# Partition sums of the sub-norms and of five row norms: from TensorE to GpSimd

## The chip, the cores and the metric

The kernel runs on one core of one Trainium2 chip. The metric is the device time of an execution in microseconds. A run is one execution; the times before are those of three runs, and the profile is of one more execution.

## What is computed

One layer of a decoder with 1024 tokens (rows) of width 2048. It is cut here to what the change touches; the projections, the stick-breaking heads and the rotary embedding are left out.

```python
def rmsnorm(x, g, eps=NORM_EPS):
    xf = x.astype(jnp.float32)
    y = xf * lax.rsqrt(jnp.mean(xf * xf, axis=-1, keepdims=True) + eps)
    return (y * g.astype(jnp.float32)).astype(x.dtype)
...
    hn = rmsnorm(h, norm_mix_g[i])
    proj = hn @ w_in[i]
...
    df_out = differential_attention(dq, dk, df_v.reshape(B, S, DF_HEADS, DF_V_DIM), lam)
    df_out = rmsnorm(df_out, subln_g[i], SUBLN_EPS) * (1.0 - lambda_init)
...
    h = h + mixed @ w_out[i]
    gate = jax.nn.sigmoid(rmsnorm(h, norm_ple_g[i]) @ w_ple_gate[i])
    h = h + gate * (p[i] @ w_ple_proj[i])
return rmsnorm(h, norm_final_g)
```

The norm behind the attention (the sub-norm) is over the 128 values of one head; the three row norms are over the 2048 values of a row.

## The kernel before

Data lies transposed: a tile has 128 features on the partitions and 512 tokens (a half of the sequence) on the free dimension. So a sum over the features of a token is a sum over partitions. Every product is done with operands split into a high and a low part (`F32R`), as three matmuls: high x high, high x low, low x high. Low parts are made by DVE as `value - high`, after ACT has cast the value to its high part.

The stages, in order: the value and gate projections of all heads (class `Seven`, `gv`); then 32 units, 16 heads for the first half of the tokens (`half = 1` in the code) and 16 for the second (`half = 0`). Differential and stick-breaking heads alternate, so there are 8 differential heads in each half. A unit projects q and k of its head (L295 to L297) while the attention of the head before runs between these matmuls. Then the output projection (`op`), the gate projection and the embeddings, and the last norm.

TensorE's instructions are kept in the order in which the program writes them; so are those of ScalarE and VectorE from L867 on. Where the attention's steps fall among the matmuls of a unit is set by the table `TICK` (L41): `side.tick()` (L264) advances one tick for each three matmuls and runs what is due. Weights for the products of `Seven` are made ahead into a ring of ten tiles (`WRING`, L654). GpSimd (POOL) issues DMAs, among them the stores of low weight parts of the first half (L197), and does a few small operations; it takes them one after the other.

The sums over partitions are products with `onesr`, a 128x128 matrix of 1/128 (L87 to L89), which leave the mean of the 128 partitions on every partition:

- Sub-norm of a differential head: `squared` (L567) squares the head's output on ACT and makes the high part `sqh`; `low` (L576) makes the low part `sql` on DVE. Some ten ticks later `norm` (L585) does two matmuls into `msq`, then `roots` takes the logarithm and the exponential on ACT and `step` refines on DVE. 8 heads, 2 halves.
- First row norm: `split_sum`, `total`, `root` and `refined` (L1153 to L1180) at slots given in `joint` (L1191), one for each half.
- Norm ahead of the gate, and the last norm of one half: the rows' squares are collected in DRAM, `load_sums` (L1938) reads them, `norm` (L1918) sums over partitions; three times (L2013, L2093, L2222).
- The last norm of the other half uses `ones` in `mean` and `mean_t` (L2282, L2289).

`scale_rope` (L1304) multiplies the tables of the rotary embedding by the row norm, on DVE for the first half and on POOL for the second.

## Time and profile before

| what | value |
|---|---|
| median of 3 runs | 2303.81 us (2303.38 to 2305.9) |
| the profiled execution, its own time | 2303.42 us |
| span of that execution | 2301.2 us |
| busy: PE, DVE, ACT, POOL | 99%, 79%, 58%, 14% of the span |
| instructions on PE, POOL | 10945, 500 |
| DMA, mean | 246 GB/s |

Busy time of PE is a modelled one, since matmuls are pipelined: the recorded durations of matmuls overlap, and the distance between starts is what one costs. Spans on POOL are rough. In the rows below PE is TensorE, DVE VectorE, ACT ScalarE and POOL GpSimd; L588 is line 588 of the kernel; times are in us, those of a single operation in the tile and line views in ns.

### The profile page before, as it was taken

The numbers are of one execution on the slowest core, as the hardware profiler recorded it, in microseconds if no ns is written. First come the engines' busy times: TensorE is split into PE (matmuls) and PEld (weight loads), VectorE is DVE, ScalarE is ACT, GpSimd is POOL, SyncE is SP. The second block draws the span as 40 slices with busy tenths as digits, with TensorE's granted clock in tenths as the row PEclk, the third lists the DMA queues.
The fourth block names the chain that finished last, engine by engine and source line by source line (L and its number), as shares of the span: only waits on it lengthen the run. The fifth ranks groups of instructions, "written<-read, shape, count | busy, mean of one in ns | idle before, by whom it ended". The sixth has DMA issues, their size and how long they took to land. (4 is left out here: it accounts for less than half of the span.)

```text
span 2301.2 us, 32625 instructions
## 1 busy us (share of the span) xinstructions
PE 2286.1 (99%) x10945; PEld 1914.5 (83%) x10945; DVE 1817.6 (79%) x3155; ACT 1337.4 (58%) x2418; POOL 322.1 (14%) x500
## 2 busy tenths in 40 slices
PE   9999999999999999999999999999999999999998
PEld 7888888888888888888888888888888888888887
DVE  6588887777768888878777878778787988687787
ACT  6424354444467777778777777777633435532555
POOL 2121111111211111101011001111121121111000
PEclk9999999999999999999999999999999999999999
DMA  7687677776798888899677667778898788998975
GB/s 268 212 303 262 209 246 228 235 216 197 236 298 260 245 257 249 258 293 307 202 207 201 170 219 210 202 211 247 249 220 247 248 247 276 320 355 267 303 254 188
DMA packets 291260, 565.06 MB, mean 246 GB/s; under 512 B 63746, under 2 KB 74242, under 8 KB 291092
## 3 DMA queue, kind: packets, MB, share of 16 engines
q1 hardware_dynamic: 220276, 383.35, 52.6%
q0 software_dynamic: 58864, 158.10, 25.1%
q10 hardware_dynamic: 11952, 21.53, 2.6%
q8 instruction: 86, 1.41, 0.3%
q14 instruction: 82, 0.67, 0.1%
HBM read 359.17 MB, written 203.69 MB: 245 GB/s over the span
## 5 line engine op out<-in xcount | busy, mean ns | idle before, releaser
L805 ACT CAST wpr<-T 128x512 fp32r<-128x512 f32 x208 | 127.6, 620 | 428.2 <-DVE T L764 363.2
L295 PE MATMUL acc<-xh,whi 128*128 128x512 f32 x768 | 309.7, 403 | 0.0
L296 PE MATMUL acc<-xl,whi 128*128 128x512 f32 x768 | 300.6, 391 | 0.0
L297 PE MATMUL acc<-xh,wlo 128*128 128x512 f32 x768 | 300.5, 391 | 0.0
L297 PEld LDWEIGHTS acc<-xh,wlo 128*128 128x128 f32 x768 | 144.2, 188 | 31.3
L295 PEld LDWEIGHTS acc<-xh,whi 128*128 128x128 f32 x768 | 144.7, 188 | 25.1
L296 PEld LDWEIGHTS acc<-xl,whi 128*128 128x128 f32 x768 | 144.8, 189 | 24.2
L805 ACT CAST wpr<-wraw 128x512 fp32r<-128x512 f32 x128 | 78.5, 617 | 120.7 <-DMA wraw<-w_vg 36.1
L819 DVE TENSOR_TENSOR wpr<-T,wpr 128x512 fp32r<-128x512 f32 x208 | 142.4, 684 | 5.9 <-ACT wpr L805 5.1
L200 ACT CAST whi<-wraw 128x1024 fp32r<-128x1024 f32 x128 | 134.1, 1048 | 11.1 <-DMA wraw<-w_in 7.1
L520 DVE TENSOR_TENSOR awl<-tp,awh 128x256 fp32r<-128x256 f32 (+1 forms) x160 | 92.6, 579 | 36.2 <-ACT awh L515 35.6
L443 ACT ACTIVATE et<-z,mx 128x512 f32<-128x512 f32 (+7 forms) x128 | 95.0, 742 | 39.1 <-DVE mx L435 38.5
L435 DVE CUSTOM_DVE_ANT_0 z<-z,wide 128x512 f32<-128x512 f32 (+7 forms) x128 | 97.6, 764 | 25.0 <-PE z L388 22.8
L710 PE MATMUL pbc<-cA,wpr 128*128 128x512 f32 x480 | 115.6, 390 | 0.2 <-DVE u L1256 0.2
L710 PE MATMUL pc<-cS,wpr 128*128 128x512 f32 x480 | 115.3, 389 | 0.0
L710 PE MATMUL pbc<-cS,wpr 128*128 128x512 f32 x480 | 115.3, 389 | 0.0
L710 PEld LDWEIGHTS pbc<-cA,wpr 128*128 128x128 f32 x480 | 90.0, 188 | 19.7 <-DVE u L1256 1.1
L710 PEld LDWEIGHTS pc<-cS,wpr 128*128 128x128 f32 x480 | 90.1, 188 | 18.7
L710 PEld LDWEIGHTS pbc<-cS,wpr 128*128 128x128 f32 x480 | 90.1, 188 | 18.7
L710 PE MATMUL pbc<-cS2h,wpr 128*128 128x512 f32 x320 | 105.3, 390 | 0.0
L710 PE MATMUL pc<-cS4h,wpr 128*128 128x512 f32 x320 | 105.0, 389 | 0.0
L918 POOL DMA_DIRECT2D vg_d<-hc x96 | 62.5, 651 | 291.1 <-DVE hc L1144 163.4
(555 smaller groups left out, 6453.0 us busy)
## 6 DMA issues: line engine op xcount, KB each, us to landing
wraw<-w_in SPq DMA_DIRECT2D x128, 512.0 KB, 5.0
wraw<-w_vg SPq DMA_DIRECT2D x143, 256.0 KB, 3.9
wlo_d<-wlo POOLq DMA_DIRECT2D x56, 512.0 KB, 6.6
vg_d<-hc POOLq DMA_DIRECT2D x96, 256.0 KB, 4.3
wlo<-wlo_d SPq DMA_DIRECT2D x48, 512.0 KB, 3.9
wraw<-w_gate SPq DMA_DIRECT2D x92, 256.0 KB, 5.3
h_d<-hc POOLq DMA_DIRECT2D x56, 256.0 KB, 5.3
wraw<-w_out SPq DMA_DIRECT2D x56, 256.0 KB, 4.5
```

Source lines behind the costliest of these rows:

```text
L200: side.later(1, lambda: A.copy(hi[:, o], raw[:, o]))
L295: T.matmul(acc[c], hi[:, k2, kh, c, :], xh, start=first, stop=False)
L296: T.matmul(acc[c], hi[:, k2, kh, c, :], xl, start=False, stop=False)
L297: T.matmul(acc[c], lo[k2][:, kh, c, :], xh, start=False, stop=last)
L435: V.tensor_tensor_reduce(z[:, vw], z[:, vw], add, -DF_SCALE, 3.0e38, ALU.add, ALU.min, mx)
L443: A.activation(et[:, vw], z[:, vw], AF.Exp, bias=mx[:, 0:1], scale=-1.0, accum_out=l[:, c:c + 1])
L520: V.tensor_tensor(wl[:, o, :], tp[:, o, :], wh[:, o, :].bitcast(F32), op=ALU.subtract)
L710: T.matmul(o, a[:, w], x, start=start and k + i == 0, stop=k == 3 and i == 2, skip_group_check=True)
L805: A.copy(t[:, 0], src)
L819: V.tensor_tensor(t[:, 1], src, t[:, 0].bitcast(F32), op=ALU.subtract)
L918: G.dma_start(vg_d[hf, blk, u], o, **(dict(accum_op=ALU.add) if ph else {}))
```

## The change

The squares of a head's output, the sums of squares of the first row norm and those of three later row norms go as they are to `partition_all_reduce` on POOL, which leaves the sum on every partition of a tile in SBUF. No high and low parts are made of them, and the scale by 1/128 moves into the logarithm and the refinement. The mean of the last norm's other half (`mean`, `mean_t`) stays on TensorE. `scale_rope` runs on DVE for both halves. `TICK` and the slots are the same, but for `total`, which stands where `split_sum` stood (slots 71 and 72).

```diff
--- before.py
+++ after.py
@@ -6,6 +6,7 @@
 import numpy as np
 
 import concourse.bass as bass
+import concourse.bass_isa as bass_isa
 import concourse.tile as tile
 from concourse import mybir
 from concourse import bacc as _bacc
@@ -18,6 +19,7 @@
 AF = mybir.ActivationFunctionType
 ALU = mybir.AluOpType
 AX = mybir.AxisListType
+RED = bass_isa.ReduceOp
 
 P = 128
 D = 2048
@@ -569,32 +571,27 @@
                 sq = ev.tile([P, HALF], F32, name="sqv", tag="xt", bufs=4)
                 A.activation(sq, both, AF.Square)
                 V.scalar_tensor_tensor(sg, both, subg[:, 0:1], sg, op0=ALU.mult, op1=ALU.mult)
-                sqh = ev.tile([P, HALF], F32R, name="sqh", tag="xt", bufs=4)
-                A.copy(sqh, sq)
-                sqs[0] = both, sq, sqh
-
-            def low():
-                both, sq, sqh = sqs[0]
-                sql = ev.tile([P, HALF], F32R, name="sql", tag="xt", bufs=4)
-                V.tensor_tensor(sql, sq, sqh.bitcast(F32), op=ALU.subtract)
-                sqs[0] = both, sq, sqh, sql
+                sqs[0] = both, sq
+
+            def summed_squares():
+                both, sq = sqs[0]
+                msq = ev.tile([P, HALF], F32, name="msq", tag="xt", bufs=4)
+                G.partition_all_reduce(msq, sq, P, RED.add)
+                sqs[0] = both, sq, msq
 
             side.later(tk("squared")[0], squared)
-            side.later(tk("squared")[1], low)
+            side.later(tk("squared")[1], summed_squares)
 
         def norm():
-            rs_, t, sqh, sql = sqs[0]
-            msq = pp.tile([P, HALF], F32, name="msq", tag="t")
-            T.matmul(msq, onesr, sqh, start=True, stop=False)
-            T.matmul(msq, onesr, sql, start=False, stop=True)
+            rs_, t, msq = sqs[0]
 
             def roots():
-                A.activation(rs_, msq, AF.Ln, bias=eps5[:, 0:1], scale=1.0)
+                A.activation(rs_, msq, AF.Ln, bias=eps5[:, 0:1], scale=1.0 / P)
                 A.activation(rs_, rs_, AF.Exp, scale=-0.5)
 
             def step():
-                V.scalar_tensor_tensor(t, msq, SUB_EPS, rs_, op0=ALU.add, op1=ALU.mult)
-                V.scalar_tensor_tensor(t, t, -0.5, rs_, op0=ALU.mult, op1=ALU.mult)
+                V.scalar_tensor_tensor(t, msq, SUB_EPS * P, rs_, op0=ALU.add, op1=ALU.mult)
+                V.scalar_tensor_tensor(t, t, -0.5 / P, rs_, op0=ALU.mult, op1=ALU.mult)
                 V.scalar_tensor_tensor(rs_, t, 1.5, rs_, op0=ALU.add, op1=ALU.mult)
                 V.tensor_tensor(sg, sg, rs_, op=ALU.mult)
                 mixed(half, hd, sg)
@@ -1148,23 +1145,16 @@
             else:
                 vput(o, ph, hf, blk, u)
 
-        rstds, halves, totals = {}, {}, {}
-
-        def split_sum(hf):
-            high, low = halves[hf] = [ev.tile([P, HALF], F32R, name=nm, tag="xt", bufs=4) for nm in ("ssah", "ssal")]
-            A.copy(high, ssa[hf])
-            V.tensor_tensor(low, ssa[hf], high.bitcast(F32), op=ALU.subtract)
+        rstds, totals = {}, {}
 
         def total(hf):
-            ps = totals[hf] = pp.tile([P, HALF], F32, name="ssps", tag="acc", bufs=2)
-            high, low = halves[hf]
-            T.matmul(ps, onesr, high, start=True, stop=False)
-            T.matmul(ps, onesr, low, start=False, stop=True)
+            totals[hf] = ev.tile([P, HALF], F32, name="total", tag="xt", bufs=4)
+            G.partition_all_reduce(totals[hf], ssa[hf], P, RED.add)
 
         steps = {}
 
         def root(hf):
-            A.activation(ssa[hf], totals[hf], AF.Ln, bias=eps6[:, 0:1], scale=1.0 / NK)
+            A.activation(ssa[hf], totals[hf], AF.Ln, bias=eps6[:, 0:1], scale=1.0 / D)
             A.activation(ssa[hf], ssa[hf], AF.Exp, scale=-0.5)
             rstds[hf] = ssa[hf]
 
@@ -1173,9 +1163,9 @@
                 steps[hf] = ev.tile([P, HALF], F32, name="nt", tag="xt", bufs=4)
             t, ps, r = steps[hf], totals[hf], ssa[hf]
             if i == 0:
-                V.scalar_tensor_tensor(t, ps, EPS * NK, r, op0=ALU.add, op1=ALU.mult)
+                V.scalar_tensor_tensor(t, ps, EPS * D, r, op0=ALU.add, op1=ALU.mult)
             elif i == 1:
-                V.scalar_tensor_tensor(t, t, -0.5 / NK, r, op0=ALU.mult, op1=ALU.mult)
+                V.scalar_tensor_tensor(t, t, -0.5 / D, r, op0=ALU.mult, op1=ALU.mult)
             else:
                 V.scalar_tensor_tensor(r, t, 1.5, r, op0=ALU.add, op1=ALU.mult)
 
@@ -1188,7 +1178,7 @@
                 rturned[hf] = const.tile([P, 4], F32, name=f"rturned{hf}", tag=f"rturned{hf}")
                 nc.sync.dma_start(rturned[hf], r_d[hf].rearrange("(j p) -> p j", p=P))
 
-        joint = {71: partial(split_sum, 1), 72: partial(split_sum, 0), 74: lambda: (total(1), total(0)), 75: partial(root, 1)}
+        joint = {71: partial(total, 1), 72: partial(total, 0), 75: partial(root, 1)}
         joint.update({76 + i: partial(refined, 1, i) for i in (0, 2)})
         joint[77] = lambda: (refined(1, 1), root(0))
         joint.update({79 + i: partial(refined, 0, i) for i in range(3)})
@@ -1302,7 +1292,7 @@
             return cs
 
         def scale_rope(hf, cs):
-            (V if hf else G).tensor_tensor(cs, cs, rstds[hf].unsqueeze(1).to_broadcast([P, 2, HALF]), op=ALU.mult)
+            V.tensor_tensor(cs, cs, rstds[hf].unsqueeze(1).to_broadcast([P, 2, HALF]), op=ALU.mult)
 
         for hf in range(2):
             rcols[hf] = const.tile([P, 2, 4], F32, name=f"rcol{hf}", tag=f"rcol{hf}")
@@ -1917,20 +1907,17 @@
 
         def norm(tiles):
 
-            out, high, low = tiles
-            ps = pp.tile([P, HALF], F32, name="ssps", tag="t")
-            T.matmul(ps, onesr, high, start=True, stop=False)
-            T.matmul(ps, onesr, low, start=False, stop=True)
+            out, ps = tiles[0], tiles[2]
 
             def roots():
                 A.preload_act_table_set("natural_log_exp_and_others")
-                A.activation(out, ps, AF.Ln, bias=eps6[:, 0:1], scale=1.0 / NK)
+                A.activation(out, ps, AF.Ln, bias=eps6[:, 0:1], scale=1.0 / D)
                 A.activation(out, out, AF.Exp, scale=-0.5)
 
             def step():
                 t = at.tile([P, HALF], F32, name="nt", tag="sg", bufs=3)
-                V.scalar_tensor_tensor(t, ps, EPS * NK, out, op0=ALU.add, op1=ALU.mult)
-                V.scalar_tensor_tensor(t, t, -0.5 / NK, out, op0=ALU.mult, op1=ALU.mult)
+                V.scalar_tensor_tensor(t, ps, EPS * D, out, op0=ALU.add, op1=ALU.mult)
+                V.scalar_tensor_tensor(t, t, -0.5 / D, out, op0=ALU.mult, op1=ALU.mult)
                 V.scalar_tensor_tensor(out, t, 1.5, out, op0=ALU.add, op1=ALU.mult)
 
             op.soon.extend([(op.slot + 1, roots), (op.slot + 2, step)])
@@ -1938,15 +1925,14 @@
         def load_sums(half, tags):
             r = []
             for i, (pool, tag, n) in enumerate(tags):
-                r.append(pool.tile([P, HALF], (F32, F32R)[i], name="sums", tag=tag, bufs=n))
-                nc.sync.dma_start(r[i].bitcast(F32), sq_d[half, i])
+                r.append(pool.tile([P, HALF], F32, name="sums", tag=tag, bufs=n))
+                nc.sync.dma_start(r[i], sq_d[half, i])
 
             def split():
-                total, high = r
-                V.tensor_tensor(total, total, high.bitcast(F32), op=ALU.add)
-                r.append(at.tile([P, HALF], F32R, name="suml", tag="sg", bufs=3))
-                A.copy(high, total)
-                V.tensor_tensor(r[2], total, high.bitcast(F32), op=ALU.subtract)
+                total, more = r
+                V.tensor_tensor(total, total, more, op=ALU.add)
+                r.append(at.tile([P, HALF], F32, name="mean", tag="sg", bufs=3))
+                G.partition_all_reduce(r[2], total, P, RED.add)
 
             op.soon.append((op.slot + TICK["sumlag"], split))
             return r
```

On POOL, at the first differential head of the first half (`msq` is the sum, `sqv` the squares, `wlo_d` the store of low weight parts, `k_d`, `kl_d` and `v_d` stores of keys and values). Before:

```order
L483 DMA v_d<-v 128x1024
L1610 DMA v_10751<-v_d 128x1024
L197 DMA wlo_d<-wlo 128x1024 x3
L1513 DMA k_d<-k 256x1x512
L1515 DMA kl_d<-kl 128x512
L197 DMA wlo_d<-wlo 128x1024 x2
L483 DMA v_d<-v 128x1024
L1513 DMA k_d<-k 256x1x512
L197 DMA wlo_d<-wlo 128x1024
```

And now:

```order
L485 DMA v_d<-v 128x1024
L1600 DMA v_10701<-v_d 128x1024
L199 DMA wlo_d<-wlo 128x1024 x2
L579 ISA msq<-sqv 128x512
L199 DMA wlo_d<-wlo 128x1024
L1503 DMA k_d<-k 256x1x512
L1505 DMA kl_d<-kl 128x512
L199 DMA wlo_d<-wlo 128x1024 x2
L485 DMA v_d<-v 128x1024
L1503 DMA k_d<-k 256x1x512
L199 DMA wlo_d<-wlo 128x1024
```

The reduction stands ahead of the last of three stores of low weight parts, and with it ahead of the stores of keys that follow.

On DVE, in the same place (`lead` and `awl` are the low parts of the attention weights that PE reads next, `wlo` the low weight part of the projection). Before:

```order
L1592 TENSOR_TENSOR qk<-qk,cs 128x512
L1579 TENSOR_TENSOR q<-qk,q 64x512
L398 TENSOR_TENSOR z<-z,masks 128x128
L579 TENSOR_TENSOR sql<-sqv,sqh 128x512
L1593 TENSOR_TENSOR qk<-qk,sw 128x512
L196 TENSOR_TENSOR wlo<-wraw,whi 128x1024
L1579 TENSOR_TENSOR q<-qk,q 64x512
L418 SCALAR_TENSOR_TENSOR pt<-pt 128x255
L519 TENSOR_TENSOR lead<-tp,lead 128x128
L520 TENSOR_TENSOR awl<-tp,awh 128x256
```

And now:

```order
L1582 TENSOR_TENSOR qk<-qk,cs 128x512
L1569 TENSOR_TENSOR q<-qk,q 64x512
L400 TENSOR_TENSOR z<-z,masks 128x128
L1583 TENSOR_TENSOR qk<-qk,sw 128x512
L198 TENSOR_TENSOR wlo<-wraw,whi 128x1024
L1569 TENSOR_TENSOR q<-qk,q 64x512
L420 SCALAR_TENSOR_TENSOR pt<-pt 128x255
L521 TENSOR_TENSOR lead<-tp,lead 128x128
L522 TENSOR_TENSOR awl<-tp,awh 128x256
```

The subtraction for `sql` is gone; the rest keeps its order. On ACT the cast for `sqh` goes in the same way, and the logarithm of `msq` stands where it stood.

On PE, at the same head, before:

```order
L387 MATMUL z<-k,q 128x512
L388 MATMUL z<-kl,qz 128x512
L588 MATMUL msq<-sqh,onesr 128x512
L589 MATMUL msq<-sql,onesr 128x512
L295 MATMUL acc_6239<-xh_5573,whi 128x512
L296 MATMUL acc_6239<-xl_5574,whi 128x512
```

The two rows with `onesr` are gone now, and their neighbours follow each other.

## Rows read from the trace of the kernel before

**Rows 1.** The page, first part: busy time, share of the span, instructions of each engine.

```profile
PE 2286.1 (99%) x10945; PEld 1914.5 (83%) x10945; DVE 1817.6 (79%) x3155; ACT 1337.4 (58%) x2418; POOL 322.1 (14%) x500
```

**Rows 2.** Waits of PE: line, waited for, us in total, times, longest.

```profile
PE av L543 <- DVE awl L520: 1.9, 4, 0.9
```

**Rows 3.** Tiles msq and ssps: count, ns min/median/max, first and last start, shape.

```profile
L588 PE MATMUL msq<-sqh,onesr x16: 389/389/501, 711.9 to 1659.3; 128*128 128x512 f32 x16
...
L1922 PE MATMUL ssps<-sums,onesr x3: 389/389/390, 1959.0 to 2208.4; 128*128 128x512 f32 x3
...
L1161 PE MATMUL ssps<-ssah,onesr x2: 389/389/389, 296.4 to 296.8; 128*128 128x512 f32 x2
```

**Rows 4.** Timeline of PE around a pair: start, us, engine, line, operation.

```profile
1164.10 0.39 PE L588 MATMUL msq<-sqh,onesr 128*128 128x512 f32 x1
...
1164.55 0.39 PE L295 MATMUL acc<-xh,whi 128*128 128x512 f32 x1
```

**Rows 5.** Lines 1305, 475, 1324 and 197, each by itself: count, ns min/median/max.

```profile
L1305 POOLq MODIFY_POOL_CONFIG  x2: 37/37/37, 1029.0 to 1029.1; - x2
...
L1305 DVE TENSOR_TENSOR cs<-cs,ssa x1: 1216/1216/1216, 635.0 to 635.0; 128x1024 f32<-128x1024 f32 x1
...
L475 POOL COPY vw<-vf x2: 778/998/1218, 1040.9 to 1041.6; 128x512 uint16<-128x512 uint16 x2
...
L1324 DVE SCALAR_TENSOR_TENSOR xl<-xl,gvec,xh x16: 719/749/851, 1030.3 to 1061.2; 128x512 fp32r<-128x512 f32 x16
...
DMA to landing us min/median/max: 4.8/6.6/9.3
```

**Rows 6.** Timeline of POOL: its add, and its two copies; idle time before, releaser.

```profile
1035.82 2.41 POOL L1305 TENSOR_TENSOR cs<-cs,ssa 128x1024 f32<-128x1024 f32 x1 [6.78 <-DMA cs<-rope]
...
1040.93 1.89 POOL L475 COPY vw<-vf 128x512 uint16<-128x512 uint16 x2 [1.51 <-PE msq L589]
```

**Rows 7.** Timeline of DVE in the same stretch.

```profile
1037.92 0.85 DVE L1324 SCALAR_TENSOR_TENSOR xl<-xl,gvec,xh 128x512 fp32r<-128x512 f32 x1 [1.36 <-ACT xh L1323]
...
1041.34 0.85 DVE L1324 SCALAR_TENSOR_TENSOR xl<-xl,gvec,xh 128x512 fp32r<-128x512 f32 x1 [0.72 <-ACT xh L1323]
```

**Rows 8.** Timeline of ACT, first differential head of the first half.

```profile
698.38 0.64 ACT L570 ACTIVATE sqv<-avb 128x512 f32<-128x512 f32 x1
...
712.83 0.69 ACT L592 ACTIVATE avb<-msq,eps 128x512 f32<-128x512 f32 x1
```

**Rows 9.** Timeline of DVE, the same head.

```profile
698.85 0.69 DVE L1579 TENSOR_TENSOR q<-qk,q 64x512 fp32r<-64x512 f32 x1
...
700.39 0.68 DVE L1593 TENSOR_TENSOR qk<-qk,sw 128x512 f32<-128x512 f32 x1
...
703.57 0.27 DVE L519 TENSOR_TENSOR lead<-tp,lead 128x128 fp32r<-128x128 f32 x1
```

**Rows 10.** Timeline of PE, the same head.

```profile
703.89 0.51 PE L538 MATMUL av<-lead,v 128*128 128x256 f32 x2
```

**Rows 11.** Timeline of ACT, first differential head of the second half.

```profile
1152.88 0.63 ACT L570 ACTIVATE sqv<-avb 128x512 f32<-128x512 f32 x1
...
1164.75 0.69 ACT L592 ACTIVATE avb<-msq,eps 128x512 f32<-128x512 f32 x1 [1.16 <-PE msq L589]
```

**Rows 12.** Timeline of DVE, the same head.

```profile
1159.80 0.81 DVE L422 TENSOR_TENSOR bt<-pt,bt 128x639 f32<-128x639 f32 x1
...
1162.68 0.69 DVE L520 TENSOR_TENSOR awl<-tp,awh 128x512 fp32r<-128x512 f32 x1 [2.06 <-ACT awh L515]
```

**Rows 13.** Timeline of PE, the same head.

```profile
1166.15 0.28 PE L543 MATMUL av<-awl,v 128*128 128x256 f32 x1
```

**Rows 14.** Timeline of POOL, first half: a store of a low weight part.

```profile
702.50 0.53 POOL L197 DMA_DIRECT2D wlo_d<-wlo  x1 [7.71 <-DVE wlo L196]
```

**Rows 15.** Timeline of DVE, first half: the later write of the low part.

```profile
712.96 1.23 DVE L196 TENSOR_TENSOR wlo<-wraw,whi 128x1024 fp32r<-128x1024 f32 x1
```

## The prediction

> **What bounds the kernel now.** I read the page's first part before anything else: TensorE (PE) is busy 2286.1 us of a span of 2301.2 us, VectorE (DVE) 79%, ScalarE (ACT) 58%, GpSimd (POOL) 14% [rows 1]. Then the waits of PE: ten rows of a few tenths to 1.9 us, and the largest is a wait for a DVE operation [rows 2]. So nothing holds PE back by more than some microseconds in all; a matmul taken out of its order shortens the kernel by that matmul, as long as whatever takes its place does not make PE wait. The profiled execution took 2303.42 us, 0.39 under the median of the runs, 2303.81. The sum below is made against 2303.4, and I take a change of under 0.2% (4.6 us) as no change, about what a measurement of this kernel can tell.
>
> **What is removed.** The tile views name the matmuls with the matrix of ones: 16 pairs for the sub-norms (L588 and L589: 8 heads, twice), 3 pairs for the row norms (L1922, L1923) and 2 pairs for the first ones (L1161, L1162) [rows 3]. That is 42 matmuls of 512 columns. Their recorded 389 ns overlap each other; what one costs PE is the distance to the next start. From the first of a pair at 1164.10 to the matmul behind the pair at 1164.55 there are 0.45 us for two [rows 4], so 0.23 us each with the rounding of the rows, and 42 x 0.23 = **9.7 us** off PE. The order listing confirms that these 42 are gone and that nothing comes in their place on PE. The 21 casts on ACT and 21 subtractions on DVE that made the high and low parts go too. They gain nothing by themselves: neither engine is the bound [rows 1, 2].
>
> **What is added.** 21 reductions over partitions on POOL, 128x512 in float32, which I call R, with a duration T. No row of the trace shows one, so T is bounded by the compute operations that POOL does have. One add of 128x1024 took 2.41 us [rows 6], so 1.2 us for 512 columns, and the faster of two copies of 128x512 took 0.78 us [rows 5]. Lower bound: R reads and writes its data once at the rate of that add, T = 1.2. Upper bound: 128 partitions are 2^7, and R does seven rounds of a move and an add, 7 x (1.2 + 0.8) = 14.0. I take seven adds with the moves hidden, T = **8.4**: it lies nearest to the add's row, which is the only float32 row, and a tree of seven steps is the least arithmetic that 128 values need one after another. The Trainium skill's page "GPSIMD Engine Reference", section 3.2, gives 247,699 ns for a reduction along the partition axis of 128x2048, another instruction than R; a quarter of it, an estimate of 61.9 us, would make the sum below some 880 us, and no row here shows it.
>
> **What else moves.** The scaling of the rope tables for the second half goes from POOL to DVE: 1.22 us there, as its twin of the first half shows [rows 5], at a place where DVE sat idle 1.36 us [rows 7]; nothing, and 1.2 us if that idle time has moved. The code load that POOL did before its add (L1305's MODIFY_POOL_CONFIG, at 1029.0 [rows 5]) now stands ahead of the first R, near 286 us. Its price is between 0 and the 6.8 us that POOL sat idle behind it, an idle time whose releaser was a DMA [rows 6]; I take 0, since the row blames the DMA.
>
> **Where R stands in time.** In the first half (seven of the eight heads, and the eighth behind the seam alike) the squares end at 698.38 + 0.64 = 699.0, and the logarithm that needs the sum stands on ACT at 712.83 [rows 8]: 13.8 us. In the second half the squares end at 1153.5, the logarithm is at 1164.75 [rows 11]: 11.2 us. With T = 8.4 the result is in time in both, so ACT does not wait. What remains is what R does to its neighbours while it runs.
>
> **The neighbour that decides: DVE.** Three rows around 1040 us show POOL and DVE in each other's way. The operation at L1324 reads two tensors from SBUF and takes 0.749 us in the median of 16; the two that started while POOL computed are the longest, 0.85 [rows 5, 7]. The first began 0.31 us before POOL's add ended, the second inside POOL's pair of copies [rows 6]. Of these two equal copies one took 778 ns and one 1218 [rows 5], and the DVE operation ends at 1042.19, 0.6 us ahead of the pair's end at 1042.82: the longer copy looks as if it had waited for DVE. So a read by POOL and a DVE operation with two SBUF inputs seem to take turns, each for its whole length. The Trainium skill's page "SBUF — State Buffer", section "Who interferes with whom", says just that: the pair of ports that both use is an exclusive lock, a VectorE instruction with two SBUF inputs contends with a GpSimd instruction that reads SBUF, and the one that starts second blocks fully. By that rule R, if it reads as it goes, stops such DVE operations for all of T. Without the rule the sum would be the 9.7 us gained and nothing else.
>
> First half: the operation at L1579, with two SBUF inputs, ends at 699.54, and R gets its turn. The next such operation, L1593, stands at 700.39 (a little earlier now, without the subtraction ahead of it), and from its start to the end of the lead tile's low part at 703.57 + 0.27 = 703.84 DVE needs 3.45 us [rows 9]. PE takes that tile at 703.89 [rows 10]: there is no slack. If L1593 starts only at 699.54 + T, PE is late by 699.54 + T + 3.45 - 703.89 = T - 0.9, so 7.5 us for T = 8.4, and 8 x 7.5 = **60 us**. The bounds: 8 x 0.3 = 2.4 at T = 1.2, and 8 x 13.1 = 105 at T = 14.0.
>
> Second half: R starts at 1153.5 and ends at 1161.9. The next DVE operation with two inputs that bears on PE is L422 at 1159.80 (0.81 us); behind it stands the low part at 1162.68 (0.69 us) [rows 12], which PE reads at 1166.15 [rows 13]. L422 at 1161.9 gives a low part that is done by 1161.9 + 0.81 + 0.69 = 1163.4: in time, **0**. At T = 14.0 it is done at 1169.0, 2.9 late, 8 x 2.9 = 23.
>
> The five R of the row norms: between 0 and 5 x 7.5 = 38. I take 0, because weight parts for those products are made ahead, in a ring of ten tiles.
>
> **Queued behind R on POOL** stand DMA issues. In the second half it is the load of keys for a later head. In the first half it is the store of low weight parts at 702.50 [rows 14], which lands 6.6 us later in the median [rows 5], and whose buffer DVE overwrites at 712.96 [rows 15]. The store may start as late as 712.96 - 6.6 = 706.4, so R may take 706.4 - 699.0 = 7.4. At T = 8.4 it is 1.0 late; that lies inside the 7.5 by which PE is late anyway, and adds nothing.
>
> **Sum.** -9.7 + 60 + 0 = +50.3, so 2303.4 + 50.3 = **2354 us**. Its own range by the bounds of T (from 3, where it starts to be distinct, -9.7 + 8 x 2.1 = +7, to 14.0, -9.7 + 105 + 23 = +118) is 2310 to 2421.
>
> **Rivals.** *Hidden (0.38).* R copies its input to memory of its own, or reads in short pieces between which DVE gets its turn, and T stays under 7.4. Then only the 9.7 us count: 2303.4 - 9.7 = **2294**. For it speaks that POOL is idle 86% of the span [rows 1] and that the largest damage that a DVE row shows is 0.1 us [rows 5, 7]; against it, that no POOL read in the trace is longer than 2.41 us, so that a wait of that kind had no occasion. This is the side opposite to my forecast, and its deciding point is what DVE's operations with two inputs do under R: unchanged, or held.
>
> *Late, with the ports free (0.10).* T is long, DVE is not held. At T = 14.0 the store at 702.50 starts at 713.0, lands at 719.6, and DVE is held 6.7 us at L196, 8 x 6.7 = 53; in the second half the logarithm is 14.0 - 11.2 = 2.8 late on ACT, with the casts for PE queued behind it, 8 x 2.8 = 22. 2303.4 - 9.7 + 53 + 22 = **2369**. It decides from T = 7.4 (store) and 11.2 (logarithm).
>
> *Break-even (0.12).* DVE is held, but T is 1.5 to 2.7: 8 x (T - 0.9) is 4.8 to 14.4 against 9.7, **2299 to 2308**.
>
> That the change does not do what it says is left out: the order listing shows the 42 matmuls gone and the 21 R there.
>
> **How the numbers follow.** Forecast 0.40, hidden 0.38, late 0.10, break-even 0.12. The forecast is only a little likelier than hidden: its mechanism has rows behind it, but how R reads its input has none. Faster 0.38, the same 0.12, slower 0.40 + 0.10 = 0.50. The range runs from hidden with some rounding on the 0.23 us, 2291, to the forecast at the upper bound of T, 2425; what it leaves out is a T far above 14.
>
> **What would show it.** PE's instruction count must fall by 42. If I am right, the profile after shows PE waits in the first half for DVE's lead and low weight parts, some 7 us per head, behind a long L1593 or a long idle time of DVE ahead of it, and none in the second half. If the rival is right, L1324-like durations stay at 0.75 us under R, and the span falls by 9.7. If ACT's logarithm is what waits, in both halves, R is longer than 11 us. I am wrong altogether if DVE's operations are unchanged and the time still rises, or if R takes under 2 us.

## The result, and the profile after

The changed kernel takes 2306.79 us in the median of 18 runs (2304.0 to 2310.15), the kernel before 2303.6 in the median of 18 beside it: ratio 1.0015, 95% interval 1.0008 to 1.0022, so 3.2 us slower. By the bound of the prediction, 0.2%, that is no change, though the interval leaves out 1; the forecast was 2354. The profiled execution took 2306.0 us.

The page's first part (busy time, share of the span, instructions), against [rows 1]:

```profile
span 2304.2 us, 32562 instructions
...
PE 2276.3 (99%) x10903; PEld 1906.3 (83%) x10903; DVE 1828.9 (79%) x3135; ACT 1326.4 (58%) x2397; POOL 393.0 (17%) x520
```

PE has 42 instructions less and is busy 9.8 us less, as the sum said; yet the span is 3.0 us longer. What took its place are waits. The waits of PE (line, waited for, us in total, times, longest), against [rows 2]:

```profile
PE av L540 <- DVE lead L521: 9.7, 9, 1.5
PE av L545 <- DVE awl L522: 3.2, 6, 1.4
PE pbc L707 <- DVE u L1246: 1.1, 2, 0.9
PE z L389 <- ACT et L445: 1.1, 1, 1.1
```

All rows of PE's timeline that carry a wait add up to 18.92 us (25 of them), against 5.96 (13) before: 12.96 more, less the 9.7 that the matmuls took, is 3.3. By place:

| place | before, us | after, us |
|---|---|---|
| heads 1 to 7 of the first half, for `lead` | 0 | 7.8 |
| between the halves (after: at 1056 and 1059.5) | 0.2 | 2.4 |
| at 330 (behind the first row norm) | 0 | 0.9 |
| last heads of the second half (after: 1585 to 1676) | 2.0 | 3.9 |
| elsewhere | 3.7 | 3.9 |

The list counts a wait from the recorded end of the matmul before it, and holds none under 0.15 us; by the distance of starts a wait costs somewhat more, as the first experiment shows. The 0.9 at 330 is no steady cost of the change: seven of the runs below make the same reductions of the first row norm and list no wait there.

The largest entry, at the first head. Timeline of PE (start, us, engine, line, operation, in brackets the wait), against [rows 10]:

```profile
705.19 0.50 PE L540 MATMUL av<-lead,v 128*128 128x256 f32 x2 [1.05 <-DVE lead L521]
```

Timeline of DVE there, against [rows 9]:

```profile
699.04 0.69 DVE L1569 TENSOR_TENSOR q<-qk,q 64x512 fp32r<-64x512 f32 x1
699.65 0.28 DVE L400 TENSOR_TENSOR z<-z,masks 128x128 f32<-128x128 f32 x1
699.97 2.41 DVE L1583 TENSOR_TENSOR qk<-qk,sw 128x512 f32<-128x512 f32 x1
...
704.87 0.27 DVE L521 TENSOR_TENSOR lead<-tp,lead 128x128 fp32r<-128x128 f32 x1
```

The reduction there, in POOL's timeline:

```profile
699.35 3.48 POOL L579 PARTITION_ALL_REDUCE msq<-sqv  x1 [4.36 <-ACT sqv L572]
```

And all 16 of that line (count, ns min/median/max, first and last start):

```profile
L579 POOL PARTITION_ALL_REDUCE msq<-sqv x16: 3233/3558/3749, 699.4 to 1652.7; - x16
```

So a reduction takes 3.2 to 3.75 us, and the addition L1583, which reads two tensors from SBUF, takes 2.41 instead of 0.68. It ends at 702.38, so its own work began at 701.70: 2.35 us behind the start of the reduction, but 1.1 before its end. I call this time of 1.73 us, by which the addition is longer, a hold. This is the mechanism of the forecast, at an eighth of its price by the listed waits. The same reduction in the second half hits nothing that matters; its DVE rows:

```profile
1161.86 0.69 DVE L522 TENSOR_TENSOR awl<-tp,awh 128x512 fp32r<-128x512 f32 x1
1163.83 0.29 DVE L398 TENSOR_TENSOR zm<-z,masks 128x128 f32<-128x128 f32 x1 [1.27 <-PE z L387]
1164.15 0.30 DVE L400 TENSOR_TENSOR z<-z,zm 128x128 f32<-128x128 f32 x1
```

There the reduction runs from 1161.18 to 1164.93. The low part L522 reads `tp` from PSUM and `awh` from SBUF, and keeps its 0.69 us inside the time in which L1583 was held.

### The profile page after: what moved, and what is told of

The parts are those of the page before. It is cut to its first block, busy times and chain, and to the rows that moved or that the text cites. A ratio compares the mean times of both kernels' runs of the same rounds, so it can differ in the third digit from the quotient of the medians.

```text
span 2304.2 us, 32562 instructions
## 1 busy us (share of the span) xinstructions
PE 2276.3 (99%) x10903; PEld 1906.3 (83%) x10903; DVE 1828.9 (79%) x3135; ACT 1326.4 (58%) x2397; POOL 393.0 (17%) x520
## 4 chain that ended last, share of the span: by engine, by line
PE 86%; DVE 7%; DMA 3%; issue 2%; ACT 2%; SPq 0%; DVEq 0%; ACTq 0%
PE pbc L707 13%; PE pa L707 9%; PE pc L707 9%; PE acc L297 9%; PE acc L299 9%; PE acc L298 9%; PE pb L707 4%; PE tp L498 2%; PE pb L1901 1%; PE pb L1902 1%; PE pb L1900 1%; PE z L390 1%; PE av L545 1%; PE z L389 1%; PE av L544 1%
## 5 line engine op out<-in xcount | busy, mean ns | idle before, releaser
L816 DVE TENSOR_TENSOR wpr<-T,wpr 128x512 fp32r<-128x512 f32 x208 | 147.8, 711 | 5.9 <-ACT wpr L802 5.2
L522 DVE TENSOR_TENSOR awl<-tp,awh 128x256 fp32r<-128x256 f32 (+1 forms) x160 | 92.6, 579 | 35.3 <-ACT awh L517 34.7
```

Source lines behind the costliest of these rows:

```text
L522: V.tensor_tensor(wl[:, o, :], tp[:, o, :], wh[:, o, :].bitcast(F32), op=ALU.subtract)
L816: V.tensor_tensor(t[:, 1], src, t[:, 0].bitcast(F32), op=ALU.subtract)
```

## The experiments

Each run was timed in 5 rounds beside the kernel before; ratios are to that kernel, with a 95% interval. PE's waits are summed as above.

### Is it the hold? The reduction somewhere else

The square on ScalarE, and so the reduction, comes 10 ticks later in the first half:

```diff
...
-            side.later(tk("squared")[0], squared)
-            side.later(tk("squared")[1], summed_squares)
+            shift = 10 if half else 0
+            side.later(tk("squared")[0], weighted)
+            side.later(tk("squared")[0] + shift, squared)
+            side.later(tk("squared")[1] + shift, summed_squares)
```

> The changed kernel, in which the square of a head of the first half, and with it the reduction, comes 10 ticks later on ScalarE (behind the casts of the keys, near 707 instead of 698.5), where VectorE next has scores from PSUM, a scan and idle time; the weighting on VectorE stays where it was. The reduction is as long as before and still stands on GpSimd ahead of stores. Theory (what costs is the hold of VectorE's operations with two SBUF inputs during the reading part of the reduction): L1583's operation is back at 0.68, the waits of PE for lead of the first half go, 2306.8 - 7.8 = 2299.0. Rival one (the reduction delays by its time on GpSimd's queue, the stores behind it): the waits move to other places, 2305 to 2309. Rival two (the logarithm now waits for the sum): PE waits of over 1 us for ScalarE behind the logarithm, 2303 to 2310.

Measured: 2296.53 us, ratio 0.9969 (0.9957 to 0.9980): 10 us faster than the change as it was, 7 faster than the kernel before. All waits for `lead` in heads 1 to 7 are gone. DVE and POOL at the first head, each in its timeline:

```profile
706.78 0.30 DVE L400 TENSOR_TENSOR z<-z,zm 128x128 f32<-128x128 f32 x1
707.57 1.97 DVE L420 TENSOR_TENSOR_SCAN pt<-pt 128x127 f32<-128x127 f32 x1 [0.49 <-ACT pt L413]
709.65 0.29 DVE L424 TENSOR_TENSOR bt<-pt,bt 128x127 f32<-128x127 f32 x1
709.88 0.56 DVE L559 TENSOR_REDUCE sm<-av 128x128 f32<-128x384 f32 x1
```

```profile
706.24 0.53 POOL L199 DMA_DIRECT2D wlo_d<-wlo  x1 [0.44 <-DVE wlo L198]
707.03 3.23 POOL L582 PARTITION_ALL_REDUCE msq<-sqv  x1 [0.26 <-ACT sqv L576]
```

The reduction still holds DVE: the scan, whose two inputs are in SBUF, takes 1.97, where the scan of this size takes 0.41 elsewhere (at 1035.75). It is released 2.1 us after the reduction's start and 1.1 before its end. But behind it some 1.1 us of idle time are still left, so nothing is late. The hold is the cause; its place is the price. Both rivals fall.

The gain is 2.5 more than the 7.8 expected, because the listed waits fall short of what the change had lost. The starts of PE's matmuls show it. In the changed kernel the one ahead of `lead` starts at 703.74, then come 705.19 and 705.53: 1.45 and 0.34 apart. Here, against [rows 10]:

```profile
757.13 0.39 PE L299 MATMUL acc<-xh,wlo 128*128 128x512 f32 x1
757.36 0.40 PE L540 MATMUL av<-lead,v 128*128 128x256 f32 x2
757.59 0.28 PE L543 MATMUL av<-awh,v 128*128 128x256 f32 x1
```

These three starts are 0.23 apart. So each of six heads of the change lost 1.22 + 0.11 = 1.33 us, where the list has 1.05, and the seventh 1.80: 9.8 in all. The period of a head agrees: 55.41 us in the change, 54.09 here. In the kernel before, two rows beside that of [rows 10] are

```profile
703.57 0.39 PE L297 MATMUL acc<-xh,wlo 128*128 128x512 f32 x1
...
704.23 0.29 PE L541 MATMUL av<-awh,v 128*128 128x256 f32 x1
```

There the starts are 0.32 and 0.34 apart: 0.2 us of waiting in each of the same six heads, too short for the list. It is gone here with the subtraction L579 of the kernel before, 0.69 us of DVE ahead of `lead`, and it is back (0.33 and 0.34) in the run below that makes the sums of the first half on PE again. The period before was 54.76 us, so a head gains 0.7 here, where the pair alone is 0.45.

### Twice the hold

```diff
-                G.partition_all_reduce(msq, sq, P, RED.add)
+                for _ in range(1 + half):
+                    G.partition_all_reduce(msq, sq, P, RED.add)
```

> The changed kernel, in which each reduction of the first half runs twice into the same tile. The second one stands on GpSimd behind the store of a low weight part, so it starts near 704.4. Theory (the reading part of a reduction, some 2.1 us, stops VectorE's operations with two SBUF inputs): the next such one, L424 for bt, is held until 706.6, 1.2 late, and PE transposes that tile with a slack of about 0.4 us: 0.8 to 1.3 per head, 2306.8 + 8 x 1.0 = 2315, with L424 recorded as 1.5 to 2.0 us long instead of 0.41. Rival (only GpSimd's queue counts; nothing PE needs soon stands behind the second one): 2306.8 to 2308.

Measured: 2332.53 us, ratio 1.0128 (1.0114 to 1.0142), 26 slower than the change. POOL's second reduction at the first head, and DVE's rows there:

```profile
704.29 3.18 POOL L580 PARTITION_ALL_REDUCE msq<-sqv  x1
```

```profile
704.15 2.86 DVE L420 TENSOR_TENSOR_SCAN pt<-pt 128x255 f32<-128x255 f32 x1
706.94 0.26 DVE L521 TENSOR_TENSOR lead<-tp,lead 128x128 fp32r<-128x128 f32 x1
```

I had the scan slip in ahead of the second reduction; it is recorded from 0.14 before it, but was held: 2.86 instead of 0.69. It stands ahead of `lead`, so PE waits 3.2 us there in six heads and 2.9 in the seventh, 14.5 more than in the change. Most of the rest came with TensorE's clock, whose granted mean over the span was 0.993 here, and 0.999, near its upper level of 2.4 GHz, in the change and in the run above. Stretches of PE before and behind its wait at 822.4, the third of these waits (columns: length, busy time of PE, PEld, DVE, ACT and POOL with instructions, granted clock, DMA share, GB/s):

```profile
815.00:822.40 7.40, 4.23 (x19) 3.12 (x18) 7.31 (x7) 4.90 (x10) 6.38 (x3) 0.94 0.53 124
822.40:830.00 7.60, 7.57 (x27) 6.54 (x28) 5.06 (x10) 2.29 (x7) 1.95 (x4) 0.61 0.91 282
830.00:838.00 8.00, 8.00 (x40) 6.73 (x39) 5.32 (x9) 6.42 (x11) 0.53 (x1) 1.00 0.27 59
```

After 3.21 us without a matmul the granted clock averages 0.61 of 2.4 GHz, near the lower level of 1.2, and the head's period goes from 57.6 to 60.3 us. The first two waits of the same length did not do this: in the 7.6 us behind each of the seven waits, the granted clock was 1.00, 1.00, 0.61, 0.78, 0.62, 0.78 and 0.59.

### Half the columns

```diff
-                G.partition_all_reduce(msq, sq, P, RED.add)
+                for c in (slice(0, 256), slice(256, 512)) if half else (slice(0, 512),):
+                    G.partition_all_reduce(msq[:, c], sq[:, c], P, RED.add)
```

> The changed kernel, in which each reduction of the first half is made as two, of 256 columns each. If a reduction's time is proportional to its columns, each takes 1.7 us and holds VectorE 1.1 us; VectorE's addition L1583 gets its turn between them, the two holds add up to about the one before: 2306 to 2308. If a large part is fixed, each takes 2.5 to 3.2 us, the holds add up to 1.5 to 2 times the one before: 2306.8 + 8 x 1.0 to 2.1 = 2315 to 2324.

Measured: 2303.63 us, ratio 0.9999 (0.9990 to 1.0008), 3 faster than the change and below both expected ranges. DVE at the first head:

```profile
700.41 1.26 DVE L1584 TENSOR_TENSOR qk<-qk,sw 128x512 f32<-128x512 f32 x1
701.59 1.21 DVE L198 TENSOR_TENSOR wlo<-wraw,whi 128x1024 fp32r<-128x1024 f32 x1
702.84 1.47 DVE L1570 TENSOR_TENSOR q<-qk,q 64x512 fp32r<-64x512 f32 x1
```

The two holds are 0.58 and 0.78, together 1.36 against 1.73 in one piece; DVE's 1.21 us between them run unhindered, and PE waits 0.7 instead of 1.05. The split reductions are in this row, with the eight whole ones of the second half:

```profile
L580 POOL PARTITION_ALL_REDUCE msq<-sqv x24: 1792/2730/3750, 699.8 to 1649.8; - x24
```

The shortest reduction of 256 columns is recorded at 1.79 us, that of 512 in this run at 3.23: the time goes with the columns, and by an estimate from these two some 0.35 us are fixed (2 x 1.79 - 3.23).

### What the reductions cost beside the hold

In the first run the sub-norms of the first half are sums on PE again, in the second all sub-norms lose their sum.

```diff
...
-            side.later(tk("squared")[1], summed_squares)
+            side.later(tk("squared")[1], low if on_pe else summed_squares)
...
```

> The changed kernel, in which the sub-norms of the first half are sums on PE again, by pairs of matmuls, as in the kernel before; those of the second half and the row norms stay on GpSimd. Theory: the waits for lead of the first half go (7.8), and 8 pairs come back (8 x 0.45 = 3.6): 2306.8 - 7.8 + 3.6 = 2302.6, so 1.0 under the kernel before; the second half keeps its own gain. Rival (the loss is not in the first half's reductions, but somewhere on GpSimd's queue or in the row norms): 2306.8 + 3.6 = 2310.4.

Measured: 2300.58 us, ratio 0.9986 (0.9977 to 0.9995). The waits for `lead` in heads 1 to 7 are gone with the reductions; the rival falls. The median is 6.2 below the change's, the profiled span 4.0, where 4.2 was expected (the profiled execution is the longest of the eleven).

```diff
-                msq = ev.tile([P, HALF], F32, name="msq", tag="xt", bufs=4)
-                G.partition_all_reduce(msq, sq, P, RED.add)
-                sqs[0] = both, sq, msq
+                t = ev.tile([P, HALF], F32, name="msq", tag="xt", bufs=4)
+                sqs[0] = both, t, sq
```

> The changed kernel without any sum over partitions in the 16 sub-norms: neither reductions nor matmuls; the refinement takes the squares themselves (this part of the computation is left out). The row norms stay on GpSimd. Theory (beside the holds, 7.8 in the first half by the waits and 10.3 by the run with the later square, and 0.5 in the seventh head of the second half, the reductions of the sub-norms cost nothing): as fast as the run with the later square less 0.5, 2296.0. Rival (they also cost by GpSimd's queue, its stores or the buffers they take, wherever they stand): 2290 to 2293.

Measured: 2295.13 us, ratio 0.9964 (0.9952 to 0.9976). Without any reduction of the sub-norms the kernel is as fast as with all 16, eight of them at a place with idle time (0.9969, intervals overlap). GpSimd's queue, the stores behind the reductions and their tiles cost nothing that can be measured.

### The scaling of the rope tables

Three runs move it: in the changed kernel back to GpSimd, the same with the later square, and in the kernel before to VectorE.

```diff
-            V.tensor_tensor(cs, cs, rstds[hf].unsqueeze(1).to_broadcast([P, 2, HALF]), op=ALU.mult)
+            (V if hf else G).tensor_tensor(cs, cs, rstds[hf].unsqueeze(1).to_broadcast([P, 2, HALF]), op=ALU.mult)
```

> The changed kernel with one thing undone: the scaling of the rope tables of the second half of the tokens is on GpSimd again. Theory (of 13.0 us of new PE waits, 7.8 come from VectorE held by the reductions of seven heads of the first half, 2.2 from this scaling, which now stands on VectorE in a tight place at 1049.75, ahead of the sub-norm's refinement and of the maxima that PE's scores wait for): the waits of PE at 1056 (1.1, for et) and 1059.5 (1.3, for lead) shrink to 0.2 in all, span 2.0 to 2.2 shorter than the changed kernel's, so 2304.6 against its 2306.8. Rival (the waits at 1056 and 1059.5 are a late consequence of the held VectorE of the seventh head, and the scaling is free as I had predicted): no change, 2306.8.

Measured: 2307.59 us, ratio 1.0015 (1.0006 to 1.0024), as the change. The waits at 1056 and 1059 are 1.73 and 0.47, hardly less: GpSimd now makes its addition only at 1050.04, in the middle of the sub-norm's refinement. The run can't tell the two theories apart, since the operation came back at another place.

> Both edits together: the later square and reduction in the first half, and the scaling of the rope tables on GpSimd. If the two causes are separate, the gains add: 2306.8 - 7.8 - 2.2 = 2296.8, 6.8 faster than the kernel before. If they are one cause, it equals the run with the later square alone, 2299.0.

Measured: 2309.39 us, ratio 1.0023 (1.0014 to 1.0032), 13 slower than with the later square alone; both expectations fall. ScalarE and PE between the halves:

```profile
1050.98 0.72 ACT L594 ACTIVATE avb<-msq,eps 128x512 f32<-128x512 f32 x1 [12.94 <-POOL msq L582]
```

```profile
1053.56 0.79 PE L297 MATMUL acc<-xh,whi 128*128 128x512 f32 x1 [12.09 <-ACT qk L1529]
```

POOL's timeline, the addition and the reduction that follows it:

```profile
1035.71 2.88 POOL L1300 TENSOR_TENSOR cs<-cs,ssa 128x1024 f32<-128x1024 f32 x1 [11.09 <-DMA wraw<-w_in]
...
1047.70 3.25 POOL L582 PARTITION_ALL_REDUCE msq<-sqv  x1 [7.76 <-issue]
```

And the code load of the reduction's line:

```profile
L582 POOLq MODIFY_POOL_CONFIG  x2: 109/112/114, 1040.1 to 1040.2; - x2
```

The change has such rows at one place, 268.8; this run has them at three, 268.7, 1024.6 and 1040.1, the second ahead of the addition and the third ahead of the reduction that follows it. So the addition needs other code on GpSimd than the reduction, and each change of it is a load: 7.5 us from the one at 1040.2 to the reduction at 1047.70, which waited for nothing else that the profile shows. Addition and load together put that reduction at 1047.70, where the run with the later square alone has it at 1033.04. The Trainium skill's page "GPSIMD Engine Reference", section 2.1, gives about 6 us for the first call of freshly loaded code; this row shows somewhat more. Such a row doesn't always cost this: in the run below with the row norms on PE, where GpSimd makes no addition, it stands at 707.8 ahead of the first reduction, which starts at 707.94. That the change put the scaling on VectorE is what keeps GpSimd on one code.

> The kernel before with one part of the change alone: the scaling of the rope tables of the second half on VectorE. Theory (1.22 us in a stretch where VectorE works without a gap; the runs without reductions in the first half still show PE waits of 1.1 and 1.3 there, against 0.24 before): PE waits 1.1 to 2.2 more, so 1.1 to 2.2 slower than the kernel before, 2304.7 to 2305.8 by its 2303.6. Rival (it is free, as I had predicted): no difference.

Measured: 2303.73 us, ratio 1.0001 (0.9992 to 1.0010). PE waits 1.31 at 1052.18 for `lead`, against 0.24 before, and the span is 0.7 longer; the median doesn't show it: alone, the scaling costs too little to be measured.

### The row norms

On the run with the later square, the five row norms are summed on PE again; and the changed kernel with all 16 sub-norms on PE.

```diff
...
-            out, ps = tiles[0], tiles[2]
+            out, high, low = tiles
+            ps = pp.tile([P, HALF], F32, name="ssps", tag="t")
+            T.matmul(ps, onesr, high, start=True, stop=False)
+            T.matmul(ps, onesr, low, start=False, stop=True)
...
```

> The run with the later square, in which the five row norms are summed on PE again, as in the kernel before; all 16 sub-norms stay on GpSimd. Theory (the row norms' 5 pairs give back 5 x 0.45 = 2.3 when they leave PE, of which 0.9 is lost at 330, where PE runs into a late DMA and the chain behind it): 2296.5 + 1.4 = 2297.9. Rival (the row norms' reductions cost nothing and save all of it): 2298.8. Second rival (they gain nothing): 2296.5.

Measured: 2297.21 us, ratio 0.9970 (0.9958 to 0.9981), against 0.9969: nearest to the second rival. The five reductions of the row norms gain nothing that can be measured; the intervals, 2.6 us to either side, don't rule out the 1.4 or the 2.3.

> The changed kernel with all 16 sub-norms summed on PE again: what is left of the change are the five reductions of the row norms and the scaling of the rope tables on VectorE. Theory (5 pairs less on PE are 2.3, of which PE loses part to later waits, 0.7 to 1.4 stay; the scaling costs 1.1 to 2.2): between 0.3 faster and 1.5 slower than the kernel before, and 0.7 to 1.4 faster than the run with the scaling alone. Rival (all of the pairs' time is gained and the scaling is free): 2.3 faster than before.

Measured: 2303.74 us, ratio 1.0002 (0.9993 to 1.0011), the same as the run with the scaling alone. PE's waits are 8.82 against 6.89 there: of the 2.3 us freed, 1.9 came back, in pieces of 0.35 to 0.6 at four places. One of these, 0.56 near 6 us, lies ahead of the first reduction, so it is not the change's. In the changed kernel the largest piece stood at 330, for `u`, and most other runs don't show it. What bounds PE at each of these places was not followed further.

### Both kernels beaten

The later square; the scaling of the tables moved on VectorE to idle time behind the score masks; the square of the seventh head of the second half, whose reduction held L688 for 1.7 us in the change, 4 ticks later. DVE in the change:

```profile
1580.63 2.40 DVE L688 TENSOR_TENSOR cA11l<-cA11l,cA11h 128x512 fp32r<-128x512 f32 x1 [1.09 <-ACT cA11h L682]
```

```diff
-    "neg": 2, "cs": 27,
+    "neg": 2, "cs": 19,
...
-            shift = 10 if half else 0
+            shift = 10 if half else 4 if hd == ORDER[-4] else 0
```

> The run with the later square, and two more places cleared: the scaling of the rope tables on VectorE comes at its tick 19 instead of 27 (behind the score masks at 1032.1, where VectorE sat idle 1.7 us), and the square of the seventh head of the second half comes 4 ticks later. Theory (each hold or added operation costs where VectorE has no idle time, and nothing where it has): the waits of PE at 1046 (1.47) and 1049.6 (1.33) fall to 0.3 in all, the one at 1575 from 1.39 to 0.9: 2296.5 - 2.5 - 0.5 = 2293.5. Rival (these waits come from the sub-norm's refinement and from GpSimd's copies of the values, not from the place of the scaling): 2296.0 to 2296.5.

Measured: 2294.27 us, ratio 0.9959 (0.9946 to 0.9973). This is 2.3 under the run with the later square alone, where 3.0 was expected and at most 0.5 by the rival; the intervals overlap. The waits at 1575 and, for the most part, at 1046 are gone; that for `lead` is still 1.33. From 1033.5 DVE works without a gap, and three of its operations are longer than their work, for which POOL's rows have the reasons: a reduction from 1032.53 and two copies from 1040.33.

```profile
1033.53 2.10 DVE L1319 SCALAR_TENSOR_TENSOR xl<-xl,gvec,xh 128x512 fp32r<-128x512 f32 x1 [0.55 <-ACT xh L1318]
...
1041.02 1.08 DVE L600 SCALAR_TENSOR_TENSOR avb<-sqv,avb 128x512 f32<-128x512 f32 x1
1042.14 1.08 DVE L601 TENSOR_TENSOR sg<-sg,avb 128x512 f32<-128x512 f32 x1
```

The copies wait for the tile of `msq` ([rows 6] name PE as releaser), and it is VectorE's refinement that releases it now, so they run beside it. So the last run gives this one head back to PE:

```diff
...
+        on_pe = half == 1 and hd == ORDER[-4]
...
```

> The run with three places cleared, in which the seventh head of the first half is summed by a pair of matmuls, because there VectorE has no idle time left (one hold of 1.35 at 1033.5, and GpSimd's copies of the values, which wait for the sum's tile, make two more VectorE operations 0.4 longer each). Theory: the waits of PE at 1044.8 (0.34) and 1048.2 (1.33) fall to 0.3 in all, and a pair comes back (0.45): 2294.3 - 1.4 + 0.45 = 2293.4. Rival (the waits there come from the mere amount of VectorE's work): 2294.7.

Measured: 2292.45 us, ratio 0.9953 (0.9941 to 0.9966), 11 us faster than the kernel before. Its span is 2290.0 us. The one wait of PE for `lead` left between the halves:

```profile
1047.61 0.50 PE L541 MATMUL av<-lead,v 128*128 128x256 f32 x2 [0.33 <-DVE lead L522]
```

PE has 40 matmuls less than in the kernel before, 40 x 0.23 = 9.2 us, and its listed waits are 6.3 against 5.96; the span is 11.2 shorter. Of the other 2 us, the six waits of 0.2 that are too short for the list make 1.2; where the rest is was not followed.

## Why the prediction was wrong

**What is removed** held for PE: 42 matmuls, 9.8 us of busy time. "They gain nothing by themselves", said of the casts and subtractions, was wrong by a little: one of the subtractions stood ahead of `lead`, and 0.2 us in each of six heads of the first half came back with it, as the starts in the run with the later square show.

**The step that failed is the size of T**, and with it the first half's term, 60 us. I took T = 8.4 as seven adds; the rows show 3.2 to 3.75. And "R stops such DVE operations for all of T" is not what happens: DVE is let go some 2.0 to 2.1 us after the reduction has its turn, 1.1 before it ends. My own rows spoke against "each for its whole length": the first L1324 in [rows 7] began 0.31 us ahead of the end of POOL's add, but was only 0.1 longer than the median.

The rest of the argument was sound. L1583 got its turn at 701.70, 2.0 behind the end of L1569 at 699.73. With 2.0 in place of T, the prediction's T - 0.9 gives 1.1 per head; six heads show 1.04 to 1.05 in the list, 1.1 more than before by the starts (1.45 against 0.32), and the seventh 1.5. The eighth, which I had counted as alike, shows none: there L1569 was held (2.62 us at 1091.78), and `lead` behind it waits for ScalarE anyway. So the term was 7.8 by the list, 8.5 by the starts (6 x 1.13, and 1.69 at the seventh), and not 60. With it alone the change would have been 1 to 2 us faster than before (9.7 less 8.5 or 7.8); what made it slower are the terms that I had set at nothing.

**The rule of the Trainium skill** that the prediction weighed, the page "SBUF — State Buffer", section "Who interferes with whom", was right in its kind: an operation with two SBUF inputs is stopped, one with a PSUM input is not, and whoever comes second waits (but for the scan of the run with two reductions, recorded from 0.14 us ahead of the reduction and held all the same). Its "for the whole instruction" is not what this reduction shows. The 61.9 us that the prediction estimated from the Trainium skill's page "GPSIMD Engine Reference", section 3.2, have no counterpart: the instruction here took a seventeenth of that.

**The second half** was right at 0 for six heads; the last two and what follows cost 1.9 us of waits, partly by the hold of L688.

**The row norms** cost nothing that shows, as I had it, but I had also counted their 5 pairs as gained, 2.3 of the 9.7, and neither pair of runs shows that gain. The **library load** at 268.8 was hidden, as taken: the first reduction waited for its input until 274.2. Such a load took 7.5 us behind an addition, and 0.1 us in the run with the row norms on PE, which has no addition on GpSimd.

**The scaling of the tables** was set at nothing for an idle time ahead of L1324. It stands elsewhere, behind the maxima, where DVE has no gap:

```profile
1049.75 1.22 DVE L1295 TENSOR_TENSOR cs<-cs,ssa 128x1024 f32<-128x1024 f32 x1
```

The order listing would have told. Alone this costs too little to measure; together with the copies that collide with the refinement, the waits between the halves grew by 2.2 in the changed kernel, and 1.1 of such waits went when the scaling moved to an idle place. The medians of the run with the later square and of the one that moved the scaling too, 2296.53 and 2294.27, also hold the move of a square in the second half (1.4 of listed waits), and their intervals overlap.

**The stores behind R** were right at 0. **The rivals:** *break-even* came out. It said that DVE is held and T is 1.5 to 2.7, for 2299 to 2308; the time is 2306.8, though its T is not met: it is DVE's being stopped that lasts 2.0 to 2.4, not T. I gave it 0.12, because I sought the bounds in T alone and not in a part of T. That R reads its input in that part would fit, but no run shows it. *Hidden* is wrong in its mechanism, since DVE is held; its 2294 is what the kernel reaches once the holds of most heads meet idle time (2294.27). The measured time lies in the stated range, 2291 to 2425, only because that range took in *hidden*: the forecast's own, 2310 to 2421, does not hold it.

## What to carry to other kernels

Before work goes to an idle GpSimd, look at what VectorE does at that moment: in these runs a reduction of 128x512 stops VectorE's operations with two SBUF inputs for 2.0 to 2.4 us, at no cost where VectorE works from PSUM or idles, and at 1.1 to 1.3 us a time where PE takes VectorE's next result without slack. Eight of the 16 reductions moved by ten ticks turned 0.15% slower into 0.3% faster, so the tick is worth a search. Work taken off a full engine counts only up to its next wait: five of the 21 pairs gave nothing that could be measured.

## What the runs showed of the hardware

- A reduction over 128 partitions, 512 columns in float32, takes 3.2 us undisturbed and up to 3.75; 256 columns 1.8. It holds VectorE for about the first two thirds only.
- The scan on VectorE is held in the same way as an addition (1.97 instead of 0.41, and 2.86 instead of 0.69). An operation with one input in PSUM kept its 0.69 under a reduction.
- On GpSimd an addition between two reductions means two code loads, one of which took 7.5 us; with the addition it put the reduction 14.7 us later and made PE wait 12.1. With no addition in the kernel, the first reduction started 0.1 us behind such a row.
- Waits of 1.05 us left TensorE's granted clock at 1.00; behind seven waits of 2.9 to 3.2 us it was 0.59 to 0.78 over 7.6 us five times, and 1.00 twice.
